# Scores of a chunked recurrence in blocks of 32 tokens: narrow diagonal products, affine maps on ScalarE, another order of heads

## The chip, the cores and the metric

The kernel runs on one core of one Trainium2 chip. The metric is device time in microseconds (us) of one execution; times are compared as medians over several runs, and each kernel also leaves one execution with a profile.

## What is computed

One layer of a decoder trunk over 1040 tokens (16 meta tokens and 1024 of the sequence) with 1024 channels in fp32: a norm, a wide projection, an HGRN2 recurrence with four heads beside a causal pooling, gates, an output projection, and a gated MLP with a causal convolution. The change lies in the recurrence. Cut to that, the reference is:

```python
f = lb + (1.0 - lb) * sigmoid(fl);  log_f = log(max(f, LOG_FLOOR))
k = (1.0 - lb) * sigmoid(-fl)
b = cumsum(log_f, axis=2)                                   # within a chunk
decay = where(causal, exp(b[t] - b[s]), 0.0)                # per channel of k
scores = einsum('bhtk,bhtsk,bhsk->bhts', q, decay, k)
o_intra = einsum('bhts,bhsv->bhtv', scores, v)
o_inter = einsum('bhtk,bhkv->bhtv', q * exp(b), state)
new_state = exp(b_last)[..., None] * state + einsum('bhsk,bhsv->bhkv', k * exp(b_last - b), v)
```

## The kernel before

Channels lie on the 128 partitions and tokens along the free axis, so a head (128 key channels) is one tile of 128x1040: q, kk (the key), f and f2 (the forget gate, twice, for a logarithm split in two ranges), b (the running sum of the logarithm, by a scan on VectorE, L632). Chunks have 128 tokens; there are NCH = 8 of them behind the meta tokens.

**Scores by levels.** A decay between two tokens must not be split into two factors that overflow. So the 128x128 causal scores of a chunk are built up by levels h = 2, 4, 8, 16, 32, 64 (LEVELS). At level h the chunk is cut into blocks of 2h tokens, and the products of a block's second half (queries) with its first half (keys) are taken, both scaled by the decay to the middle of the block. `level_in` (L669 to L681) makes the scaled tile d: a subtraction, two exponentials, two multiplies. `level_mm` (L683 to L696) multiplies: for levels 32 and 64 only the block's own quadrant, with 32 or 64 stationary columns (L691); for levels 2 to 16 the whole chunk, 128 stationary columns against the 64 queries of that level (L695), of which most products are of no use. `level_out` (L698 to L710) brings them into sc, the scores of the head (128x1024, cleared on GpSimd at L648): for levels 32 and 64 by copies (L704), below that by a copy under a mask (L710), 512 elements on each partition. The masks are made at the start (L575 to L594). Pairs of neighbouring tokens (the base, L759 to L766) come from a product of the whole chunk, 128x128 (L763), and a masked copy of 512 elements for each half of the chunks (L764).

**The steps of a head.** `head_steps` is a generator; each `h` with a number in the list ORDER runs one head on to its next yield, twelve in all: (1) the input of levels 2 and 4 and of the meta tokens, (2) meta product (L663) and level 2, (3) level 4 and the input of 8 and 16, (4) level 8, (5) level 16 and the input of 32 and 64, (6) level 32, (7) level 64 and the factors qs, kd, e1 (L726 to L745), (8) transposes of kd (L752, L755), (9) the base, (10) the states (L772 to L783), (11) scores times values and queries times state (L794 to L805), (12) the norm of the head (L809 to L817).

**The order of the work.** ORDER is a list written out by hand. F, Q, G, PV are projections of one head (or one pooling group) each, with bodies at L208 to L212 (`a` and `b` behind a letter: first and second half of the projection); after an F, `c` runs `chain_f` (L623 to L633): five element steps on VectorE (L624 to L628), two logarithms on ScalarE, an addition and the scan. `post_q` (L635) copies the queries. PP, BB and BA are the pooling and branch products, sp, sa, w smaller steps of them. Each projection's weights come through a loader three ahead, on the queue of SyncE. POOLED names the element steps that run on GpSimd instead of VectorE (such as `lq64.1`, level 64's query multiply of head 1). In this stage the order that ORDER gives is put onto the engines by the tile framework; the stages before and after (values and gates, then the output projection and the MLP) are ordered by hand. PSUM is a pool of eight banks in this stage. SBUF slots have a pitch of LP = 1088 elements.

Of the kernel before, what the change touches and what calls it, by code (L numbers as in the profile page):

```python
# [8 lines left out]
F32 = mybir.dt.float32  # L9
# [5 lines left out]
P = 128  # L15
# [25 lines left out]
LSPLIT = 2.0 ** -60  # L41
LUP = 2.0 ** 60
KT = 6
HT = 514
HN = HT - HALO
HP = 528
# [11 lines left out]
ORDER = ("F0 c0 Q0 h0 F1 h0 h0 c1 Q1 h0 h1 h0 F2 h1 h1 c2 h0 h0 Qa2 Qb2 h1 h1 h2 G2 h0 h0 h1 Fa3 h1 h2 h0 h2 Fb3 "  # L58
# [3 lines left out]
POOLED = ("e1k.0 e1k.3 kdmul.2 kdmul.3 kdsub.2 lk32.1 lk4.1 lq16.1 lq32.1 lq32.2 lq64.0 lq64.3 lq8.0 lq8.1 lq8.2 "  # L62
          "osg.2 sub2.2 sub32.1 sub8.1 wBA2 wBA6 wBA7 wBB2 wF0 wF2 wF3 wPP2 wPV0 wPV1 wQ0 wQ1 lq4.3 kdsub.1 qsmul.1 "
          "lk32.0 e1q.3 e1q.1 lq2.1 wQ2 sub2.3 rsl.0 lk32.3 lq64.1 qsmul.2").split()
TRUNC = False

CH_ALL = [(0, 348), (348, 346), (694, 346)]
# [4 lines left out]
def trunk_kernel(ctx: ExitStack, tc: tile.TileContext, x, meta_tokens, mix_norm_pre,  # L72
# [48 lines left out]
    def small(shape, name, tag, bufs=4):  # L121
        return sm.tile(shape, F32, tag=tag, name=nm(name), bufs=bufs)
# [360 lines left out]

    lb = const.tile([P, HEADS], F32, name="lb")
    oml = const.tile([P, HEADS], F32, name="oml")

    def params():
# [12 lines left out]
        dve.tensor_scalar(oml, lb, -1.0, 1.0, ALU.mult, ALU.add)  # L500


    junk_bank = bank("pj")
# [70 lines left out]

    LEVELS = (2, 4, 8, 16, 32, 64)  # L575
    masks = {}
    mbase = const.tile([P, P], U8, name="mbase")
    mtmps = slot(P + len(LEVELS) * P // 2, name="mtmps")
    mtmp = mtmps[:, :P]
    pool_e.memset(mtmp, 1.0)  # L580
# [4 lines left out]
    pool_e.tensor_copy(mbase, mtmp)  # L585
    for i, h in enumerate(LEVELS):
# [6 lines left out]
        masks[h] = const.tile([P, P // 2], U8, name=f"mask{h}")  # L593
        pool_e.tensor_copy(masks[h], mt)  # L594

    def V(c, h):
        return heads[h]["v"][:, c * P : (c + 1) * P]
# [23 lines left out]
        return lambda: chain_f(h, kk, b, f, f2)  # L621

    def chain_f(h, kk, b, f, f2):  # L623
        dve.tensor_scalar(f, f, oml[:, h : h + 1], lb[:, h : h + 1], ALU.mult, ALU.add)  # L624
        dve.tensor_scalar(kk, kk, oml[:, h : h + 1], None, ALU.mult)
        dve.tensor_scalar(f2, f, LUP, 1.0, ALU.mult, ALU.min)
        dve.tensor_scalar(f2, f2, LOG_FLOOR * LUP, None, ALU.max)
        dve.tensor_scalar(f, f, LSPLIT, None, ALU.max)  # L628
        act.activation(f2, f2, AF.Ln)
        act.activation(f, f, AF.Ln)  # L630
        eng(f"lf.{h}").tensor_tensor(f, f, f2, ALU.add)
        dve.tensor_tensor_scan(b, keep_on, f, 0.0, ALU.mult, ALU.add)  # L632
        heads[h].update(kk=kk, b=b, f=f)  # L633

    def post_q(h, pq):  # L635
        q = slot(L, name="q")
        for (lo, n), ps in zip(CH_Q, pq):
            act.copy(q[:, T0 + lo : T0 + lo + n], ps[:, :n])
        heads[h]["q"] = q

    def head_steps(h):
# [6 lines left out]
        pool_e.memset(sc, 0.0)  # L648
# [34 lines left out]
        def level_mm(lv, qk):  # L683
            ps = bank("sl")
            half = lv >= 32
            for c in range(NCH):
                t = NM + c * P
                if half:
                    for i in range(P // (2 * lv)):
                        s, n = t + 2 * lv * i, 2 * lv * i  # L690
                        pe.matmul(ps[n : n + lv, c * lv : (c + 1) * lv], qk[:, s : s + lv], qk[:, s + lv : s + 2 * lv],  # L691
                                  start=True, stop=True)
                    continue
                rhs = qk[:, t : t + P].rearrange("p (b two h) -> p b two h", two=2, h=lv)[:, :, 1, :]
                pe.matmul(ps[:, c * 64 : (c + 1) * 64], qk[:, t : t + P], rhs, start=True, stop=True)  # L695
            return ps  # L696

        def level_out(lv, ps):  # L698
            if lv >= 32:
                o3 = sc.rearrange("p (c t) -> p c t", c=NCH)  # L700
                p3 = ps[:, : NCH * lv].rearrange("p (c h) -> p c h", c=NCH)
                for i in range(P // (2 * lv)):
                    n = 2 * lv * i
                    dve.tensor_copy(o3[n : n + lv, :, n + lv : n + 2 * lv], p3[n : n + lv])  # L704
# [5 lines left out]
            dve.copy_predicated(o4, m4, p4)  # L710

# [44 lines left out]
        ktm = small([NM, P], "ktm", "ktm", 2)  # L756
        act.copy(ktm, pm[:NM, :P])
        yield
        for j in range(2):  # L759
            ps = bank("sb")  # L760
            for i in range(4):
                t = NM + (4 * j + i) * P
                pe.matmul(ps[:, i * P : (i + 1) * P], kk[:, t : t + P], q[:, t : t + P], start=True, stop=True)  # L763
            dve.copy_predicated(sc[:, j * 512 : (j + 1) * 512].rearrange("p (c t) -> p c t", c=4),  # L764
                                mbase.rearrange("p (o t) -> p o t", o=1).to_broadcast([P, 4, P]),
                                ps.rearrange("p (c t) -> p c t", c=4))  # L766
        yield


# [1031 lines left out]
```

## Time and profile before

| | us |
|---|---|
| median of 3 runs | 1330.72 (1330.1 to 1331.8) |
| the profiled execution | 1330.1 |
| its span, first to last instruction | 1328.4 |
| TensorE busy | 1317.1 |
| VectorE busy | 970.7 |
| ScalarE busy | 566.8 |
| GpSimd busy | 440.4 |

In the profile PE is TensorE's matmuls, PEld its weight loads, DVE VectorE, ACT ScalarE, POOL GpSimd, SP SyncE. A row of instructions by line reads: line, engine, operation, tile written and tiles read, shapes, how many | busy us, mean ns of one | idle us of the engine just before them, and what ended that. A row of the timeline reads: start, length, engine, line, operation, tiles, shapes, how many. A row of waits reads: who, for whom: us in total, times, longest. An fp32 matmul leaves two records. Matmuls are pipelined: the mean length of one is a latency, and the rate shows in the busy time of a row and in the starts of the timeline. The stage of the head steps runs from about 255 to 510 us.

### The profile page before, as it was taken

To read this page: it belongs to the slowest core of one execution; us is meant where nothing else is said; L and a number is where in the kernel's file an instruction comes from. 1 tells how busy PE (TensorE), PEld (TensorE's weight loads), DVE (VectorE), ACT (ScalarE), POOL (GpSimd) and SP (SyncE) were. 2 spreads that over 40 slices of the span, in tenths; PEclk is the share of its full clock that TensorE was granted. 3 is DMA by queue.
4 is the path that set the end of the run, shared out by engine and by line. 5 is a ranking of instruction groups with operands and counts; after the bars stand their busy time and mean duration, and the time that the engine had idled before them with its cause. 6 is when DMAs were issued, how large, how long until landed. Compare 5 with 4: busy or idle time off the path is not lost.

```text
span 1328.4 us, 19923 instructions
## 1 busy us (share of the span) xinstructions
PE 1317.1 (99%) x7713; PEld 1177.6 (89%) x7713; DVE 970.7 (73%) x1229; ACT 566.8 (43%) x946; POOL 440.4 (33%) x327
## 2 busy tenths in 40 slices
PE   8999999999999999999999999999999999999997
PEld 7799899999999999987898888888888888888886
DVE  6765545389968777766578999888988885455758
ACT  5553333365556575235564222322222233444443
POOL 2015421226525720061025555545555652000000
PEclk9999999999999999999999999999999999999999
DMA  7134332411011157987686776676766799666644
GB/s 272 41 110 157 124 109 99 125 50 48 19 51 35 35 170 268 350 280 257 219 300 234 183 211 188 198 205 171 178 161 142 175 246 310 215 224 223 222 174 159
DMA packets 139665, 230.38 MB, mean 173 GB/s; under 512 B 9000, under 2 KB 77196, under 8 KB 139570
## 3 DMA queue, kind: packets, MB, share of 16 engines
q1 hardware_dynamic: 127506, 204.71, 45.3%
q0 software_dynamic: 12064, 24.38, 10.8%
q8 instruction: 61, 1.00, 0.3%
q14 instruction: 34, 0.28, 0.1%
HBM read 165.56 MB, written 86.53 MB: 190 GB/s over the span
## 4 chain that ended last, share of the span: by engine, by line
PE 95%; DVE 4%; DMA 0%; ACT 0%; issue 0%; SPq 0%; DVEq 0%
PE P L311 15%; PE P L312 15%; PE P L314 15%; PE pd L188 5%; PE pd L190 5%; PE pd L189 5%; PE pm L188 2%; PE pm L189 2%; PE pm L190 2%; PE sl L695 1%; PE ppv L208 1%; PE pbb L208 1%; PE ppv L212 1%; PE pbb L209 1%; PE ppv L209 1%; PE pbb L212 1%
## 5 line engine op out<-in xcount | busy, mean ns | idle before, releaser
L312 PE MATMUL P<-v,whi 128*128 128x512 f32 (+2 forms) x408 | 140.7, 353 | 0.0
L311 PE MATMUL P<-v,whi 128*128 128x512 f32 (+2 forms) x408 | 140.7, 352 | 0.0
L314 PE MATMUL P<-v,wlo 128*128 128x512 f32 (+2 forms) x424 | 135.1, 349 | 0.0
L1535 DVE TENSOR_TENSOR rot<-wraw,rot 128x1024 fp32r<-128x1024 f32 x31 | 38.0, 1225 | 72.3 <-ACT rot L1534 72.2
L282 POOL TENSOR_TENSOR swa<-wraw,wraw 128x512 f32<-128x512 f32 x28 | 42.3, 1510 | 133.0 <-DMA wraw<-in_ffn_w_gate_dram 69.3
L311 PEld LDWEIGHTS P<-v,whi 128*128 128x128 f32 x408 | 76.7, 188 | 10.4
L312 PEld LDWEIGHTS P<-v,whi 128*128 128x128 f32 x408 | 76.6, 188 | 10.2
L314 PEld LDWEIGHTS P<-v,wlo 128*128 128x128 f32 x424 | 74.0, 188 | 10.8
L256 ACT CAST whi<-wraw 128x512 fp32r<-128x512 f32 x78 | 46.1, 618 | 87.6 <-PE P L312 64.2
L190 PE MATMUL pd<-rot 128*128 128x512 f32 x272 | 82.1, 389 | 0.0
L189 PE MATMUL pd<-rot 128*128 128x512 f32 x272 | 82.1, 389 | 0.0
L188 PE MATMUL pd<-rot 128*128 128x512 f32 x272 | 81.1, 389 | 0.1
L1534 ACT CAST rot<-wraw 128x1024 fp32r<-128x1024 f32 x31 | 32.7, 1055 | 90.8 <-PE pd L190 89.4
L256 ACT CAST whi<-swa 128x512 fp32r<-128x512 f32 x56 | 33.4, 618 | 81.9 <-PE P L312 76.2
L1463 DVE SCALAR_TENSOR_TENSOR y<-g,par,y 128x1024 f32<-128x1024 f32 x44 | 64.5, 1467 | 0.8
L257 DVE TENSOR_TENSOR wlo<-swb,whi 128x512 fp32r<-128x512 f32 x56 | 59.9, 1075 | 6.9 <-ACT whi L256 6.9
L257 DVE TENSOR_TENSOR wlo<-wraw,whi 128x512 fp32r<-128x512 f32 x74 | 62.3, 864 | 2.7 <-ACT whi L256 2.7
L256 ACT CAST whi<-swb 128x512 fp32r<-128x512 f32 x56 | 33.4, 618 | 68.6 <-PE P L312 64.2
L188 PEld LDWEIGHTS pd<-rot 128*128 128x128 f32 x272 | 51.0, 188 | 11.1 <-DVE p L1471 0.5
L189 PEld LDWEIGHTS pd<-rot 128*128 128x128 f32 x272 | 51.1, 188 | 10.6
L190 PEld LDWEIGHTS pd<-rot 128*128 128x128 f32 x272 | 51.0, 188 | 10.6
L311 PE MATMUL P<-t4h,whi 128*128 128x258 f32 (+1 forms) x196 | 57.0, 307 | 0.0
(421 smaller groups left out, 4133.0 us busy)
## 6 DMA issues: line engine op xcount, KB each, us to landing
wraw<-in_w_in_dram SPq DMA_DIRECT2D x36, 512.0 KB, 4.0
yt<-ysum SPq DMA_DIRECT2D x33, 512.0 KB, 4.5
wraw<-in_ffn_w_gate_dram SPq DMA_DIRECT2D x26, 512.0 KB, 7.3
wraw<-in_ffn_w_up_dram SPq DMA_DIRECT2D x22, 512.0 KB, 6.1
wsum<-in_ffn_w_down_dram SPq DMA_DIRECT2D x22, 512.0 KB, 9.0
wraw<-in_w_out_dram SPq DMA_DIRECT2D x18, 512.0 KB, 5.5
ysum<-ys SPq DMA_DIRECT2D x11, 768.0 KB, 7.7
sa<-sscr SPq DMA_DIRECT2D x16, 513.0 KB, 6.8
```

Of the source, the lines that this page charges most:

```text
L188: pe.matmul(ps, ahi, bhi, start=first, stop=False)
L189: pe.matmul(ps, ahi, blo, start=False, stop=False)
L190: pe.matmul(ps, alo, bhi, start=False, stop=last)
L256: act.copy(hi, src)
L257: (pool_e if 4 <= i < 2 * self.early else dve).tensor_tensor(lo, src, rr(hi), ALU.subtract)
L282: pool_e.tensor_tensor(s1, a21, a22, ALU.add)
L311: pe.matmul(d, whi[:, k, :], xh[:, c : c + w], start=(k == 0 and onto is None), stop=False, **go)
L312: pe.matmul(d, whi[:, k, :], xl[:, c : c + w], start=False, stop=False, **go)
L314: pe.matmul(x[:, o : o + w], wlo[:, k, :], xh[:, c : c + w], start=False, stop=(k == 3), **go)
L1463: dve.scalar_tensor_tensor(a, g[:, j : j + SEQ], cvw[:, j, m : m + 1], a, ALU.mult, ALU.add)
L1534: act.copy(hi, src)
L1535: dve.tensor_tensor(lo, src, rr(hi), ALU.subtract)
```

## The change

- Levels 2 to 16 and the base are taken per block of BLK = 32 tokens: for each chunk four matmuls with 32 stationary columns, their outputs on partitions 0, 32, 64 and 96, with 16 moving columns (levels) or 32 (base). The masked copies then have 128 elements (levels) or 256 (base) on each partition, and go to a tile of their own, dg (128x256, cleared on GpSimd, three buffers), from which, after the base, four copies of 32 partitions by 256 elements set the blocks onto the diagonal of sc. Three of the four copies of head 3 and all others are on VectorE; `dg1.3` is on GpSimd. The masks shrink with them.
- In chain_f the affine map of f goes to ScalarE, once plain and once scaled for f2; the multiplication of kk by 1 - lb is left out and q is scaled by it instead, in the copy out of PSUM. Two maxima and minima of f2 become one instruction.
- ORDER and POOLED change: Q2 is no longer split, PV1 is; head steps, sa and some branch products change places; `e1k.0`, `kdsub.2` and `lq64.1` go from GpSimd to VectorE. ACTED, the list of copies for ScalarE, is empty.
- The pitch LP is 1056.

```diff
+BLK = 32
-LP = 1088
+LP = 1056
-ORDER = ("F0 c0 Q0 h0 F1 h0 h0 c1 Q1 h0 h1 h0 F2 h1 h1 c2 h0 h0 Qa2 Qb2 h1 h1 h2 G2 h0 h0 h1 Fa3 h1 h2 h0 h2 Fb3 "
-         "h2 c3 h2 PVa0 h1 h1 PVb0 Q3 h1 h3 h0 h1 h2 h3 h2 h3 h1 PV1 h3 sp0 h3 sa1 PV2 h2 h2 PP0 h3 PVa3 h3 sp2 h2 "
+ORDER = ("F0 c0 Q0 h0 F1 h0 h0 c1 Q1 h0 h1 h0 F2 h1 h1 c2 h0 h0 Q2 h1 h2 G2 h1 h0 h2 h0 Fa3 h1 h0 h1 h2 Fb3 h2 c3 "
+         "h2 h1 PVa0 h1 PVb0 Q3 h1 h3 h0 h1 h2 h3 h2 h3 h1 PVa1 h3 PVb1 sp0 h3 PV2 h2 h2 PP0 h3 PVa3 sa1 h3 sp2 h2 "
...
+        dve.tensor_scalar(lbu, lb, LUP, None, ALU.mult)
+        dve.tensor_scalar(omlu, oml, LUP, None, ALU.mult)
...
-        dve.tensor_scalar(f, f, oml[:, h : h + 1], lb[:, h : h + 1], ALU.mult, ALU.add)
-        dve.tensor_scalar(kk, kk, oml[:, h : h + 1], None, ALU.mult)
-        dve.tensor_scalar(f2, f, LUP, 1.0, ALU.mult, ALU.min)
-        dve.tensor_scalar(f2, f2, LOG_FLOOR * LUP, None, ALU.max)
+        act.activation(f2, f, AF.Identity, scale=omlu[:, h : h + 1], bias=lbu[:, h : h + 1])
+        act.activation(f, f, AF.Identity, scale=oml[:, h : h + 1], bias=lb[:, h : h + 1])
+        dve.tensor_scalar(f2, f2, 1.0, LOG_FLOOR * LUP, ALU.min, ALU.max)
         dve.tensor_scalar(f, f, LSPLIT, None, ALU.max)
...
-            act.copy(q[:, T0 + lo : T0 + lo + n], ps[:, :n])
+            act.activation(q[:, T0 + lo : T0 + lo + n], ps[:, :n], AF.Copy, scale=oml[:, h : h + 1])
...
+        dg = small([P, NCH * BLK], "dg", "dg", 3)
         pool_e.memset(sc, 0.0)
+        pool_e.memset(dg, 0.0)
...
-                rhs = qk[:, t : t + P].rearrange("p (b two h) -> p b two h", two=2, h=lv)[:, :, 1, :]
-                pe.matmul(ps[:, c * 64 : (c + 1) * 64], qk[:, t : t + P], rhs, start=True, stop=True)
+                for n in range(0, P, BLK):
+                    k = qk[:, t + n : t + n + BLK]
+                    rhs = k.rearrange("p (b two h) -> p b two h", two=2, h=lv)[:, :, 1, :]
+                    pe.matmul(ps[n : n + BLK, c * BLK // 2 : (c + 1) * BLK // 2], k, rhs, start=True, stop=True)
...
-            o4 = sc.rearrange("p (c b two h) -> p c b two h", c=NCH, two=2, h=lv)[:, :, :, 1, :]
-            p4 = ps.rearrange("p (c b h) -> p c b h", c=NCH, h=lv)
-            nb = P // (2 * lv)
+            nb = BLK // (2 * lv)
+            o4 = dg.rearrange("p (c b two h) -> p c b two h", c=NCH, two=2, h=lv)[:, :, :, 1, :]
+            p4 = ps[:, : NCH * BLK // 2].rearrange("p (c b h) -> p c b h", c=NCH, h=lv)
             m4 = masks[lv].rearrange("p (o b h) -> p o b h", o=1, h=lv).to_broadcast([P, NCH, nb, lv])
             dve.copy_predicated(o4, m4, p4)
...
-        for j in range(2):
-            ps = bank("sb")
-            for i in range(4):
-                t = NM + (4 * j + i) * P
-                pe.matmul(ps[:, i * P : (i + 1) * P], kk[:, t : t + P], q[:, t : t + P], start=True, stop=True)
-            dve.copy_predicated(sc[:, j * 512 : (j + 1) * 512].rearrange("p (c t) -> p c t", c=4),
-                                mbase.rearrange("p (o t) -> p o t", o=1).to_broadcast([P, 4, P]),
-                                ps.rearrange("p (c t) -> p c t", c=4))
+        ps = bank("sb")
+        for c in range(NCH):
+            for n in range(0, P, BLK):
+                t = NM + c * P + n
+                pe.matmul(ps[n : n + BLK, c * BLK : (c + 1) * BLK], kk[:, t : t + BLK], q[:, t : t + BLK], start=True,
+                          stop=True)
+        d3 = dg.rearrange("p (c t) -> p c t", c=NCH)
+        dve.copy_predicated(d3, mbase.rearrange("p (o t) -> p o t", o=1).to_broadcast([P, NCH, BLK]),
+                            ps[:, : NCH * BLK].rearrange("p (c t) -> p c t", c=NCH))
+        for n in range(0, P, BLK):
+            r = slice(n, n + BLK)
+            o3 = sc[r].rearrange("p (c t) -> p c t", c=NCH)[:, :, r]
+            if f"dg{n // BLK}.{h}" in ACTED:
+                act.copy(o3, d3[r])
+            else:
+                eng(f"dg{n // BLK}.{h}").tensor_copy(o3, d3[r])
```

More of the change, by code (lines that the diff above doesn't have):

```diff
@@ L485, in trunk_kernel @@
     oml = const.tile([P, HEADS], F32, name="oml")
+    lbu = const.tile([P, HEADS], F32, name="lbu")
+    omlu = const.tile([P, HEADS], F32, name="omlu")
     def params():
@@ L576, in trunk_kernel @@
     masks = {}
-    mbase = const.tile([P, P], U8, name="mbase")
+    mbase = const.tile([P, BLK], U8, name="mbase")
     mtmps = slot(P + len(LEVELS) * P // 2, name="mtmps")
@@ L584, in trunk_kernel @@
                          pattern=[[2, P // 2], [1, 2]], channel_multiplier=-1)
-    pool_e.tensor_copy(mbase, mtmp)
-    for i, h in enumerate(LEVELS):
+    for n in range(0, P, BLK):
+        r = slice(n, n + BLK)
+        pool_e.tensor_copy(mbase[r], mtmp[r, r])
+    for i, h in enumerate(LEVELS[:4]):
         mt = mtmps[:, P + i * P // 2 : P + (i + 1) * P // 2]
@@ L592, in trunk_kernel @@
                              pattern=[[2 * h, P // (2 * h)], [0, h]], channel_multiplier=-1)
-        masks[h] = const.tile([P, P // 2], U8, name=f"mask{h}")
-        pool_e.tensor_copy(masks[h], mt)
+        masks[h] = const.tile([P, BLK // 2], U8, name=f"mask{h}")
+        for n in range(0, P, BLK):
+            r = slice(n, n + BLK)
+            pool_e.tensor_copy(masks[h][r], mt[r, n // 2 : (n + BLK) // 2])
     def V(c, h):
@@ L758, in head_steps @@
         yield
-        for j in range(2):
-            ps = bank("sb")
-            for i in range(4):
-                t = NM + (4 * j + i) * P
-                pe.matmul(ps[:, i * P : (i + 1) * P], kk[:, t : t + P], q[:, t : t + P], start=True, stop=True)
-            dve.copy_predicated(sc[:, j * 512 : (j + 1) * 512].rearrange("p (c t) -> p c t", c=4),
-                                mbase.rearrange("p (o t) -> p o t", o=1).to_broadcast([P, 4, P]),
-                                ps.rearrange("p (c t) -> p c t", c=4))
+        ps = bank("sb")
+        for c in range(NCH):
+            for n in range(0, P, BLK):
+                t = NM + c * P + n
[4 more added lines that the diff above has]
+                            ps[:, : NCH * BLK].rearrange("p (c t) -> p c t", c=NCH))
+        for n in range(0, P, BLK):
+            r = slice(n, n + BLK)
+            o3 = sc[r].rearrange("p (c t) -> p c t", c=NCH)[:, :, r]
[3 more added lines that the diff above has]
+                eng(f"dg{n // BLK}.{h}").tensor_copy(o3, d3[r])
         yield
```

10 lines of the change are left out of this document (6 added, 4 removed), and 4 rows, old and new, of the table ORDER.

## The prediction, made before the change was run

> **What bounds the kernel now.** I read the page first: busy times, the forty slices, the chain that ended last.
>
> ```profile
> PE 1317.1 (99%) x7713; PEld 1177.6 (89%) x7713; DVE 970.7 (73%) x1229; ACT 566.8 (43%) x946; POOL 440.4 (33%) x327
> ...
> PE   8999999999999999999999999999999999999997
> ...
> DVE  6765545389968777766578999888988885455758
> ...
> PE 95%; DVE 4%; DMA 0%; ACT 0%; issue 0%; SPq 0%; DVEq 0%
> ```
>
> TensorE (PE) is busy in every slice and carries 95% of the chain. The profiled execution took 1330.1 us around a span of 1328.4; I work against 1330.1, 0.6 under the median of the runs shown (1330.72). Since a busy PE is not a PE at its peak, the question is how densely matmuls follow each other where the change works. The busy times by stage (columns: window, length, then PE, PEld, DVE, ACT, POOL, clock, DMA share, GB/s) and PE's waits inside 255 to 470 us give:
>
> ```profile
> 255.00:280.00 25.00, 25.00 (x160) 24.89 (x158) 17.55 (x17) 12.62 (x21) 5.86 (x3) 1.00 0.23 65
> 280.00:320.00 40.00, 40.00 (x324) 39.46 (x323) 35.66 (x32) 28.37 (x46) 21.26 (x12) 1.00 0.23 67
> 320.00:360.00 40.00, 39.43 (x316) 38.51 (x314) 39.50 (x38) 23.30 (x36) 23.94 (x13) 1.00 0.05 16
> 360.00:400.00 40.00, 40.00 (x284) 39.49 (x284) 26.98 (x41) 20.17 (x37) 11.95 (x7) 1.00 0.15 42
> 400.00:440.00 40.00, 40.00 (x328) 39.54 (x327) 33.21 (x32) 25.02 (x40) 20.45 (x10) 1.00 0.09 29
> 440.00:470.00 30.00, 30.00 (x249) 29.09 (x248) 21.31 (x29) 18.17 (x32) 23.99 (x11) 1.00 0.13 38
> ```
>
> ```profile
> PE sl L691 <- ACT sg L825: 0.4, 1, 0.4
> ```
>
> This is the stage of the head steps. PE waits once, 0.4 us; the clock is granted in full. VectorE (DVE) is close behind, above all from 320 to 360 (39.50 of 40), ScalarE (ACT) and GpSimd (POOL) are not, and DMA is nearly idle. So PE's time taken out of this stage should shorten the kernel one for one, as long as DVE doesn't become what PE waits for. PE has no idle slice behind the stage in which the gain could be lost.
>
> **PE: what the change removes and adds.** Of PE's work only the scores change. Rows grouped by line and form (one fp32 matmul leaves two records):
>
> ```profile
> L695 PE MATMUL sl<-d 128*128 128x64 f32 x256 | 30.2, 274 | 0.0
> ...
> L763 PE MATMUL sb<-q,kk 128*128 128x128 f32 x64 | 8.0, 275 | 0.0
> ...
> L691 PE MATMUL sl<-d 128*32 128x32 f32 x128 | 2.8, 197 | 0.4 <-ACT sg L825 0.4
> ```
>
> L695 is levels 2 to 16: 16 groups (4 levels, 4 heads) of 8 matmuls, 16 records. L763 is the base: 4 groups of 16 records. Each group becomes 32 matmuls, so 64 records, with 32 stationary columns and 16 (levels) or 32 (base) moving ones. Four times the records, so all depends on the price of one. The mean of one, 197 ns, is a latency; the busy column shows that they overlap. The row that has almost the new form is L691 at level 32: 128x32 stationary, 32 moving, output alternating between partitions 0 and 64; only the moving width of the levels and two more output places differ. The timeline of PE gives starts, from which I take what a group occupies:
>
> ```profile
> 294.73 0.63 PE L212 MATMUL pq<-uhi,wlo 128*128 128x342 f32 x3
> 295.20 3.68 PE L695 MATMUL sl<-d 128*128 128x64 f32 x32
> 298.69 0.40 PE L208 MATMUL pf<-uhi,whi 128*128 128x348 f32 x1
> ```
>
> ```profile
> 441.70 0.65 PE L212 MATMUL ppp<-plh,wlo 128*128 128x342 f32 x3
> 442.27 0.70 PE L691 MATMUL sl<-d 128*32 128x32 f32 x32
> 442.90 0.43 PE L208 MATMUL ppv<-uhi,whi 128*128 128x348 f32 x1
> ```
>
> ```profile
> 438.98 1.95 PE L763 MATMUL sb<-q,kk 128*128 128x128 f32 x16
> 440.68 0.40 PE L208 MATMUL ppp<-plh,whi 128*128 128x342 f32 x1
> ```
>
> ```profile
> 442.27:442.77 0.50, 0.49 (x30) 0.50 (x32) 1.00 0.11 33
> ...
> 345.41:345.91 0.50, 0.49 (x31) 0.50 (x32) 1.00 0.00 0
> ```
>
> - Two old levels, 32 records, hold PE from 295.20 to 298.69: 3.49 us, 1.745 a level. An old base holds it 440.68 - 438.98 = 1.70.
> - 32 narrow records hold it 442.90 - 442.27 = 0.63. In the windows of L691 alone, 30 or 31 of them run in 0.50 us: **0.016 us a record**, the rest (about 0.12) being the way back to wide matmuls.
> - The way in: three L212 last 442.27 - 441.70 = 0.57 before the narrow group, 295.20 - 294.73 = 0.47 before the wide one, so 0.10 more.
>
> A new group standing alone: 0.10 + 0.63 + 32 x 0.016 = 1.24. Two levels side by side pay the ways in and out once: 0.10 + 0.63 + 96 x 0.016 = 2.27, or 1.13 a level. The gain is 0.50 to 0.61 a level; the groups at 295.20 and, further down, at 280.29 are pairs, so I take the middle, 0.56: 16 x 0.56 = **9.0 us**. The base: 4 x (1.70 - 1.24) = **1.8 us**. At level 2 the group follows the meta matmuls (L663), 16 columns wide, which now need no change of form behind them:
>
> ```profile
> 280.11 0.25 PE L663 MATMUL sm<-q,em 128*16 128x2 f32 x4
> 280.29 3.79 PE L695 MATMUL sl<-d 128*128 128x64 f32 x32
> ```
>
> four records hold PE 0.18 there, some 0.06 of it the way out, and the 0.10 of the way in goes too: 4 x 0.16 = **0.6 us**. Sum: 11.4 us.
>
> Can the queue feed such bursts? At 345.41 the group starts with nothing queued up (PE had just waited 0.4 us), and still 31 records start in 0.50 us; so feeding isn't the limit at this price, though a burst of 64 or 128 records isn't in the trace.
>
> Two rules of the Trainium skill bear on the price. The Trainium skill, "TensorE: Matmul & The Clock Gate", section "Wait — 56ns, not 53.3ns?", says that starts are never less than about 25 ns apart however few columns move. By it a group would be an estimated 64 x 25 ns = 1.6 us before the ways in and out, and the change would bring nothing; the trace disagrees for groups whose output alternates (0.50 us for 31). "TensorEngine Tiling (Array Packing)" of the Trainium skill, section "Theoretical Speedup", allows up to four times for 32 columns, one tile to each quarter; no run here shows four.
>
> **The other engines: cover.** DVE rows of the steps touched, and the rows that price what is new:
>
> ```profile
> L710 DVE COPY_PREDICATED sc<-mask,sl 128x512 f32<-128x512 uint8 x16 | 13.8, 863 | 6.0 <-PE sl L695 5.8
> ...
> L764 DVE COPY_PREDICATED sc<-mbase,sb 128x512 f32<-128x512 uint8 x8 | 5.8, 739 | 6.5 <-PE sb L763 6.5
> ...
> L704 DVE COPY sc<-sl 32x256 f32<-32x256 f32 x8 | 3.3, 415 | 5.3 <-PE sl L691 5.2
> ...
> L658 DVE TENSOR_TENSOR em<-em,kk 128x32 f32<-128x32 f32 x4 | 0.7, 185 | 0.3 <-ACT em L657 0.3
> ...
> L624 DVE TENSOR_SCALAR f<-f,oml,lb 128x1040 f32<-128x1040 f32 x4 | 4.6, 1141 | 13.4 <-ACT f L619 13.4
> ...
> L625 DVE TENSOR_SCALAR kk<-kk,oml 128x1040 f32<-128x1040 f32 x4 | 3.0, 752 | 0.0
> ...
> L626 DVE TENSOR_SCALAR f<-f 128x1040 f32<-128x1040 f32 x4 | 3.9, 970 | 0.0
> ...
> L627 DVE TENSOR_SCALAR f<-f 128x1040 f32<-128x1040 f32 x4 | 3.6, 910 | 0.1
> ...
> L628 DVE TENSOR_SCALAR f<-f 128x1040 f32<-128x1040 f32 x4 | 2.8, 692 | 0.0
> ...
> L731 DVE TENSOR_TENSOR kd<-b 128x1024 f32<-128x1024 f32 x2 | 2.4, 1217 | 0.0
> ...
> L745 DVE TENSOR_TENSOR kk<-kk,e 128x512 f32<-128x512 f32 x2 | 2.3, 1174 | 0.0
> ```
>
> ```profile
> L629 ACT ACT_TABLE_LOAD x4 | 5.1, 1283 | 0.1
> ...
> L630 ACT ACTIVATE f<-f 128x1040 f32<-128x1040 f32 x4 | 4.2, 1061 | 0.2 <-DVE f L628 0.2
> ```
>
> ```profile
> L648 POOL MEMSET sc<- 128x1024 f32 x4 | 3.8, 956 | 4.0 <-DVE f L631 4.0
> ```
>
> - Level masks: 128 instead of 512 elements. Between 185 (L658, 32 elements) and 863 ns; I take 300: 13.8 becomes 4.8. Base: one of 256 elements a head between the same ends, I take 420: 5.8 becomes 1.7.
> - New: 16 copies of 32x256 onto the diagonal, 15 on DVE. Priced by L704: 15 x 0.415 = 6.2.
> - Decay: L624 to L628 are 17.9 us; two maxima or minima a head remain, 8 x 0.8 = 6.4.
> - Three steps come from POOL to DVE: the kd difference of head 2 (1.2, like L731) and two multiplies of heads 0 and 1 (1.2 each, like L745): 3.6.
>
> DVE: -9.0 - 4.1 + 6.2 - 11.5 + 3.6 = about -15 us, more than PE loses. That is why I cost the change at nothing besides PE: what PE waits for moves forward further than PE does. The two affine maps go to ACT, 8 x 1.06 = 8.5 us; ACT is busy 127.6 us of these 215, so they fit; if each head's pair brought a table load of its own (L629), 4 x 1.28 = 5.1 us more of the same idle time. The scale in the copy of q is free work in an instruction that was there. POOL gains a clearing of 256 elements a head (0.24 each, a quarter of L648) and one copy and loses three steps. The clearing waits for a buffer at head 3 alone (there are three); head 0's base, which frees it, stands far ahead in the order list, so nothing is held up behind it. The one diagonal copy on POOL waits for head 3's masked base; what stands behind it there are steps of the same head's tail, late in the stage, when PE has the branch matmuls to do. SP issues the same loads, in the order of the new list, into a stage in which DMA is nearly idle. Masks and two small parameter steps stand at the start, off PE's path. In the chain from base to output, one masked copy and four copies (0.42 + 4 x 0.415 = 2.1 us) replace two masked copies (1.5): 0.6 us later per head, but the state step stands between. The reordering, taken with halves that split differently, moves the same instructions of PE, and the smaller row pitch moves nothing; a wait that these bring is a rival below. Bounds: no wait goes (0.4 at most to gain), up to a few us may come.
>
> **Rivals.**
> - *Four quarters overlap more than two.* The records of one group go to four places in turn. If twice as many run at once, 0.008 a record: a group alone is 0.10 + 0.12 + 64 x 0.008 = 0.73; gain 16 x 1.0 + 4 x 0.97 + 0.6 = 20.5 us, so **1309.6**. Against it: the two records of one matmul share a quarter and follow each other, and at level 32 they already set the pace. Chance 0.13. The second rule of the Trainium skill, above, speaks for this case.
> - *DVE takes over.* From 280 to 360, DVE works 75.2 of 80 us. If the new order needs its results sooner than the relief makes them, PE waits. If half of the gain goes that way, the time is **1325**. For: 39.50 of 40; against: DVE's own loss of work. Chance 0.13.
> - *A floor under the start of a record.* L663's four records, all to one place, take 0.18 with a way out of 0.06 to 0.12: 0.030 to 0.015 each. If the new ones have such a floor, then near its middle, at 0.024, a group costs what it did, 0.22 + 64 x 0.024 = 1.76, and the time is **1330**. Against it: 0.016 in two windows. Chance 0.06. The first rule of the Trainium skill, above, leads to this case.
> - *The quarters don't overlap at all in the new sequence* (the slower side). Then a record costs its own quarter's time, twice 0.016: a group is 0.22 + 64 x 0.032 = 2.27; 16 x 0.52 + 4 x 0.57 - 0.6 = +10 us, **1340**. It decides from (1.745 - 0.22) / 64 = 0.024 us a record on. Against it: 0.016 measured with the same columns. Chance 0.06.
>
> **How the numbers follow.** Forecast 1330.1 - 11.4 = 1318.7 against the profiled execution, 1319.3 against the median; I say **1319.3**, chance 0.62. The range, from the four-quarter case to the floor: 1310 to 1330. A measurement here tells 0.2% (2.7 us) from no change. Faster: 0.62 + 0.13 + 0.12 = 0.87; same: the floor and a little of the DVE case, 0.07; slower: 0.06.
>
> **What would show it.** Right: PE's narrow groups hold it near 1.2 us each (32 to 0.5 us), the scores' total falls by about 11 us, PE's waits between 255 and 460 stay under 1 us, DVE's busy time falls by some 15 us and ACT's rises by 8 or 9. Wrong: records over 0.024 us apart; waits of PE on masked copies, scan or level products; or records 0.008 apart, which would make the gain about double.

## The result and the profile after

The changed kernel takes **1331.89 us** (median of 20 runs, 1330.49 to 1336.51) against 1330.27 for the kernel before in the same rounds: 1.0019 times as long, interval [1.0011, 1.0027]. The forecast was 1319.3. The profiled execution is one of its longer ones: 1335.12 us, span 1333.4.

From the page of the changed kernel, the busy times, TensorE's slices and the engines' shares of the chain that ended last:

```profile
PE 1305.4 (98%) x8673; PEld 1157.9 (87%) x8673; DVE 972.5 (73%) x1234; ACT 576.0 (43%) x954; POOL 437.3 (33%) x335
...
PE   8999999998999999999999999999999999999997
...
PE 84%; DVE 7%; ACT 3%; DMA 3%; issue 2%; SPq 0%; POOL 0%; DVEq 0%; ACTq 0%
```

PE is busy for 11.7 us less and still ends later. Its share of the chain went from 95% to 84%: somewhere it is no longer PE that sets the time. The busy times by stage say where (window, length, PE, PEld, DVE, ACT, POOL, clock, DMA share, GB/s):

```profile
255.00:280.00 25.00, 25.00 (x160) 25.00 (x159) 12.81 (x13) 14.79 (x22) 6.54 (x3) 1.00 0.23 64
280.00:320.00 40.00, 33.98 (x603) 32.58 (x602) 29.95 (x30) 29.80 (x47) 19.35 (x11) 0.93 0.21 56
320.00:360.00 40.00, 38.04 (x517) 36.36 (x517) 33.20 (x39) 27.05 (x40) 17.41 (x11) 0.99 0.10 29
360.00:400.00 40.00, 36.64 (x471) 35.40 (x470) 29.05 (x39) 20.82 (x36) 13.87 (x8) 0.96 0.15 43
400.00:440.00 40.00, 38.14 (x594) 36.85 (x594) 34.39 (x37) 25.89 (x43) 19.71 (x9) 1.00 0.10 30
```

Before, PE was busy 40.00, 39.43, 40.00 and 40.00 us in the last four; now it has 6.0, 2.0, 3.4 and 1.9 us without work. No other engine is full over 40 us either, so the waits have to be read one by one. PE's waits over the whole kernel (waiting engine, tile and line, whom for: us, times, longest):

```profile
PE sl L708 <- DVE d L691: 4.8, 3, 3.4
PE pm L190 <- DVE sa L918: 3.0, 1, 3.0
PE pj L513 <- POOL ident masks.py:199: 2.0, 1, 2.0
PE sl L708 <- issue: 1.9, 2, 1.4
PE sl L702 <- DVE d L691: 1.8, 1, 1.8
PE sl L702 <- DVE d L690: 1.7, 1, 1.7
PE pf L210 <- ACT kt L767: 1.5, 1, 1.5
```

Before, the waits listed in this way were 4.0 us in all, 0.4 of them in this stage. Most of the new ones are level products (L708: levels 2 to 16; L702: 32 and 64) that wait for their input d, above all for its multiplies on VectorE (L690, L691). What the products themselves cost, and VectorE's and ScalarE's rows of the parts that changed, in the stage:

```profile
L691 DVE TENSOR_TENSOR d<-d,kk 128x512 f32<-128x512 f32 x20 | 23.2, 1164 | 5.0 <-ACT d L689 5.0
...
L690 DVE TENSOR_TENSOR d<-d,q 128x512 f32<-128x512 f32 x14 | 14.1, 1012 | 2.9 <-ACT d L688 2.9
L788 DVE COPY sc<-dg 32x256 f32<-32x256 f32 x15 | 12.9, 863 | 0.3
L708 PE MATMUL sl<-d 128*32 128x16 f32 x1024 | 12.0, 187 | 7.7 <-DVE d L691 4.8 <-issue 1.9 <-DVE d L690 1.0
...
L688 ACT ACT_TABLE_LOAD x5 | 6.4, 1283 | 0.1
...
L724 DVE COPY_PREDICATED dg<-mask,sl 128x128 f32<-128x128 uint8 x16 | 5.3, 330 | 1.8 <-PE sl L708 1.5
...
L634 ACT ACTIVATE f<-f,lbu,omlu 128x1040 f32<-128x1040 f32 x4 | 5.1, 1269 | 0.0
```

The 30.2 us of L695 became 12.0. VectorE's multiplies, for which PE waits, did not get shorter; before, they were:

```profile
L680 DVE TENSOR_TENSOR d<-d,kk 128x512 f32<-128x512 f32 x20 | 17.8, 891 | 0.1
L679 DVE TENSOR_TENSOR d<-d,q 128x512 f32<-128x512 f32 x13 | 15.6, 1203 | 0.0
```

So 33 of them took 33.4 us before, and 34 take 37.3 now. A narrow group standing alone, in PE's timeline:

```profile
421.60 0.72 PE L708 MATMUL sl<-d 128*32 128x16 f32 x64 [0.44 <-DVE d L691]
422.25 0.42 PE L214 MATMUL ppv<-uhi,wlo 128*128 128x346 f32 x1
```

and a base, which moves 32 columns:

```profile
378.20 0.76 PE L777 MATMUL sb<-q,kk 128*32 128x32 f32 x64
378.89 0.43 PE L210 MATMUL ppv<-uhi,whi 128*128 128x348 f32 x1
```

64 records hold PE 422.25 - 421.60 = 0.65 us. In such groups the first and last starts are 0.54 to 0.55 us apart, so one record takes **0.0087 us**, about half of what two places in turn took (0.016). The levels' groups also have half the moving columns of that row, but the base has all 32 and holds PE no longer to speak of (378.89 - 378.20 = 0.69 us): it is the four places, and not the smaller width, that halve the price. By such starts the sixteen wide levels and four wide bases held PE 35.3 us before (0.7 of a wait inside taken off), and the narrow ones, where nothing holds them up, 13.0: 0.67 alone, 1.24 a pair, 0.69 a base. PE's part of the gain is thus **22 us**, twice my 11.4, and none of it arrived. (The ways into the narrow form, 0.1 us each, are not in this; busy times of runs below give 21.)

One place shows how. The critical chain of the changed kernel between 281 and 320 us (start, length, what):

```profile
281.66 0.18 PE pf L211
...
284.21 0.46 ACT f L629
...
286.47 1.28 ACT L688
...
289.44 0.52 ACT d L689
289.96 1.16 ACT f L634
...
291.14 1.26 ACT f L635
...
292.42 1.28 ACT L638
...
295.78 1.25 DVE f L640
...
297.06 2.34 DVE b L641
...
302.28 3.70 DVE d L686 x2
305.99 2.23 DVE wlo L157
...
309.83 4.17 DVE d L690 x2
...
314.21 2.56 DVE d L691
...
316.90 1.94 PE sl L702 x16
```

From the end of head 1's projection (281.8) to 316.9 nothing on this chain is PE's. ScalarE does sigmoids, then, queued behind them, the exponentials of another head with a table load (L688), then the new affine maps, then a table load for the logarithms (L638); VectorE follows with sum, scan, differences, a split of weights and multiplies. Two multiplies at 309.83 take 2.1 us each, while the shortest of the same form take 0.68. PE's time around it (same columns as above):

```profile
308.00:312.00 4.00, 2.07 (x107) 1.73 (x107) 4.00 (x5) 3.46 (x6) 4.00 (x3) 1.00 0.45 131
312.00:316.00 4.00, 1.44 (x87) 1.23 (x75) 4.00 (x3) 2.37 (x6) 4.00 (x2) 0.79 0.02 4
316.00:320.00 4.00, 3.10 (x20) 3.01 (x21) 3.85 (x7) 2.08 (x4) 1.57 (x3) 0.50 0.52 140
320.00:324.00 4.00, 4.00 (x23) 4.00 (x23) 3.62 (x5) 3.94 (x5) 2.49 (x2) 0.86 0.44 122
```

VectorE is full, GpSimd works beside it, PE waits, and from about 314 to 321 the granted clock is 0.50: the waits are paid twice. "TensorE: Matmul & The Clock Gate" of the Trainium skill, section "Part 1: The HAM clock gate (the "warmup" mystery)", says that an idle window of some 3.4 us halves the clock and a busy one brings it back; the trace agrees in the lengths, with stretches at half clock of 6.8 us here and 3.4 us near 370 and 584. It doesn't quite agree in the condition: in the 3.4 us before the fall at 314 PE was not idle throughout, but ran a group of 0.73 us at 311.74.

### The profile page after: what moved, and what is told of

The parts are those of the page before. It is cut to its first block, busy times and chain, and to the rows that moved or that the text cites. A ratio compares the mean times of both kernels' runs of the same rounds, so it can differ in the third digit from the quotient of the medians.

```text
span 1333.4 us, 21871 instructions
## 1 busy us (share of the span) xinstructions
PE 1305.4 (98%) x8673; PEld 1157.9 (87%) x8673; DVE 972.5 (73%) x1234; ACT 576.0 (43%) x954; POOL 437.3 (33%) x335
## 4 chain that ended last, share of the span: by engine, by line
PE 84%; DVE 7%; ACT 3%; DMA 3%; issue 2%; SPq 0%; POOL 0%; DVEq 0%; ACTq 0%
PE P L313 15%; PE P L316 15%; PE P L314 15%; PE pd L190 5%; PE pd L191 5%; PE pd L192 5%; PE pm L190 2%; PE pm L191 2%; PE pm L192 2%; PE pv L191 1%; DVE d L686 1%; PE pv L192 1%; PE pv L190 1%; PE pq L210 1%; PE pq L211 1%
## 5 line engine op out<-in xcount | busy, mean ns | idle before, releaser
L259 DVE TENSOR_TENSOR wlo<-swb,whi 128x512 fp32r<-128x512 f32 x56 | 63.5, 1140 | 6.8 <-ACT whi L258 6.7
L258 ACT CAST whi<-swa 128x512 fp32r<-128x512 f32 x56 | 33.4, 618 | 81.2 <-PE P L314 78.3
L258 ACT CAST whi<-swb 128x512 fp32r<-128x512 f32 x56 | 33.4, 618 | 69.4 <-PE P L314 65.0
```

The lines of the kernel that those rows point to most:

```text
L258: act.copy(hi, src)
L259: (pool_e if 4 <= i < 2 * self.early else dve).tensor_tensor(lo, src, rr(hi), ALU.subtract)
```

## The experiments

I began with three theories. **P**: the shorter pitch of 1056 makes products slower that stream from SBUF. **C**: PE, quicker now, comes to the level products before VectorE has their input ready. **O**: the new order of heads makes the waits by itself. All times are medians; "before" ran beside each.

### e1, e12: the pitch

```diff
-LP = 1088
+LP = 1056
```

> The kernel before with a slot pitch of 1056 instead of 1088 and nothing else. Theory P (the pitch matters): in the changed kernel the 512-wide matmuls that read the normed input take 232 ns from start to start instead of 227, and the 1056 matmuls of the gates hold the engine 157.9 us instead of 156.7, ahead of any other part of the change; so the pitch alone should give the same 232 ns and 157.9 us and a time 2 to 4 us above the kernel before. Rival (those records were slow in that execution for another reason): 227 ns, 156.7 us, a time within 1 us.

The kernel before with this alone: **1335.81** (before 1330.16), 1.0044 [1.0032, 1.0057]. P holds, and is larger than expected: +5.6 us. Starts of 512-wide products lie 229 to 232 ns apart in place of 227 for the later tiles (t4h, t4l, zc) and 232 to 233 for the normed input; PE is busy 3.9 us longer (1321.0 against 1317.1), and its listed waits grow from 4.0 to 5.8 us in all. In e12 the normed input kept 1088:

```diff
-U0 = LP - L
+UP = 1088
+U0 = UP - L
-    def ubig(dtype, name, n=KD * LP):
+    def ubig(dtype, name, n=KD * UP):
...
```

> The kernel before with the slots of the head steps at the new pitch of 1056 columns and the normed input's tiles left at 1088: it splits the 5.6 us that the pitch of 1056 cost for both. If the cost lies with the streamed normed input (the gates' 512-wide products, 227 to 232 ns), the time is within 1.5 us of before's 1330.2. If it lies with the slots (zc, yh and yl, t1l), it is 1333 to 1336 us; evenly shared, 1332 to 1333.

**1333.19** (before 1330.31), 1.0018 [1.0009, 1.0027]: half of the cost, 2.9 us, lies with the slots, the rest with the normed input, whose products are back at 227 ns here.

### e2, e3, e4: the other parts alone

e2 has the narrow products, dg and the pitch, but the old chain_f, copy of q, ORDER and POOLED. e3 is the kernel before with the new chain_f and copy of q, e4 the kernel before with the new ORDER and POOLED; their diffs are the ones shown with the change.

> The kernel before with the narrow products alone (blocks of 32, small masks, the tile dg and its four copies, pitch 1056), with the old decay steps, the old order list and the old list of GpSimd steps. Theory C (cover): the scores' matmuls fall by some 25 us of TensorE time, and TensorE then waits for the inputs of the levels, since the list puts the products of one level right behind those of another and the wide products were the cover; time 1322 to 1334, with 15 us or more of waits between 280 and 465 us. Theory O (the new order and the moved steps make the waits): few waits, under 5 us in all, time 1305 to 1312.

> The kernel before with the decay's affine maps on ScalarE alone (and q scaled in place of kk), wide products, old order, old pitch. Theory C: TensorE hides it, within 1.5 us of the kernel before, TensorE's waits between 280 and 465 us under 1 us. Theory O: the longer way over ScalarE makes TensorE wait, 3 us slower or more.

> The kernel before with the new order list and the new list of GpSimd steps alone; wide products, old decay, old pitch. Theory C: within 2 us of the kernel before, with the wide products still covering the inputs. Theory O: 5 us slower or more, with waits of TensorE for level inputs near 310 and 366 us and for the last branch products near 580 us, as in the changed kernel.

e2: **1334.79**, 1.0028 [1.0017, 1.0040]; e3: **1330.96**, 1.0006 [0.9997, 1.0015]; e4: **1334.78**, 1.0035 [1.0022, 1.0047]. PE waits in e2 at the same kinds of places as after the change, 14.7 us between 255 and 470 against 13.7, so the narrow products bring the waits under the old order too, and O falls as the sole cause. (The pitch is in e2 as well; against e1 the narrow products alone are worth 1.0 us.) Under the wide products the affine maps cost nothing that can be told. With the wide products the new order and the new list of GpSimd steps cost 4.6 us together, between what C and O gave them: PE's listed waits are 8.5 us in e4 against 4.0 before.

### e5: the normed input's pitch given back

The diff of e12, on the changed kernel.

> The changed kernel with the old pitch of 1088 for the two big tiles of the normed input alone; all other slots keep 1056. Theory P1 (the pitch acts through the normed input's start addresses): the 512-wide matmuls that read it come back to 227 ns from 232, the gates' 1056 matmuls hold the engine 156.7 us again, and the time falls by 2 to 3 us, to about 1329.5. Rival P2 (each slot has its own part): the matmuls on other slots stay slow (zc 230, yh and yl 231 ns) and the time falls by 1 us or less.

**1330.44** (before 1330.5), 1.0004 [0.9994, 1.0013]: 1.5 us better than after by the medians, between what the two theories of its forecast gave, and the base of most of what follows.

### e6, e7, e8: is it the level inputs alone?

e6 adds the old wide products behind each narrow group, into columns that nobody reads; e7 lets the products read q in place of d, while d is still made and nothing reads it, so the scores are other ones; e8 moves halves of the projections Q2, G2 and PV0 between the head steps, on e5.

```diff
# e6
+                    pe.matmul(ps[:, 256 + (c % 4) * 64 : 320 + (c % 4) * 64], qk[:, t : t + P], rhs, start=True, stop=True)
# e7
-                level_out(lv, level_mm(lv, d))
+                level_out(lv, level_mm(lv, q))
# e8
-"F0 c0 Q0 h0 F1 h0 h0 c1 Q1 h0 h1 h0 F2 h1 h1 c2 h0 h0 Q2 h1 h2 G2 h1 h0 h2 h0 Fa3 h1 h0 h1 h2 Fb3 h2 c3 "
+"F0 c0 Q0 h0 F1 h0 h0 c1 Q1 h0 h1 h0 F2 Qa2 h1 h1 c2 h0 Qb2 h0 h1 h2 Ga2 h1 h0 Gb2 h2 h0 Fa3 h1 h0 h1 h2 Fb3 h2 c3 "
-"h2 h1 PVa0 h1 PVb0 Q3 ...
+"PVa0 h2 h1 PVb0 h1 Q3 ...
```

> The changed kernel, and behind every narrow group of levels 2 to 16 and of the base also the old wide products, into columns that nothing reads: TensorE has the old work of about 36 us again on top, while VectorE, ScalarE and GpSimd do what they do in the changed kernel. Theory C (TensorE waits for level inputs that the wide products used to cover): most of it falls into the waits, the waits between 280 and 465 us go from some 27 us to under 10 and the time rises by 6 to 16 us, to 1338 to 1348. Rival (the waits are of something that more TensorE work can't cover, such as banks or the order): the whole 36 us come on top, 1366 to 1370.

> The changed kernel, but the products of all six levels take the query tile, which is ready early, on both sides in place of the scaled tile d; d is still made in full, by the same steps, and nothing reads it. The scores are therefore not those of the reference. Theory C: the waits of TensorE for d go, the time falls by 12 to 24 us, to 1308 to 1320. Rival (the order of the steps or the throughput of VectorE sets the stage): the waits move to other operands and the time stays within 4 us of the changed kernel.

> The changed kernel with the old pitch for the normed input (as e5) and an order list that puts half a projection between head steps which stood back to back: Q2 and G2 in halves, steps of heads 0, 1 and 2 between the halves. Theory C: the waits near 310 us shrink from 6 us to 2 or less, and the time is 1320 to 1326. Rival (the chain of a head sets the stage however the projections lie, or the transfers of the branch stage do): within 3 us of e5.

e6: **1357.04**, 1.0189 [1.0174, 1.0205]; e7: **1333.93**, 1.0032 [1.0019, 1.0045]; e8: **1336.96**, 1.0043 [1.0031, 1.0056]. e6 is 25 us above the changed kernel, between the two ranges of its forecast: of the 36 us of added PE work only 11 fell into waits. That is no pure measure of the waits, since VectorE's masked copies now wait 7.7 us for the added products. In e7 the waits for d go, but PE's waits are now these:

```profile
PE pt L766 <- DVE st L804: 3.8, 1, 3.8
PE sl L702 <- DVE dg L724: 3.6, 1, 3.6
PE pm L190 <- DVE sa L918: 3.1, 1, 3.1
...
PE po L825 <- DVE st L804: 2.0, 2, 1.5
```

PE waits for banks and states that VectorE frees or makes later in its queue. e8 is 6.5 us slower than e5, which neither of its theories gave: the wait near 310 us is gone and one of 9.6 us, for kd on VectorE, stands at 331. So C in its plain form falls: whichever product is relieved, another one waits. That left **theory D**: in this stage VectorE, ScalarE and GpSimd, each in order and feeding each other, go at a pace of their own, and PE, relieved of 22 us, only waits for them.

### e9 and e16: the pace taken away

The exponentials and multiplies of the levels are left out (d holds the bare differences, so the scores are other ones), in e9 from e5, in e16 from the kernel before.

```diff
-            act.activation(db[:, :, 1, :], db[:, :, 1, :], AF.Exp)
-            act.activation(db[:, :, 0, :], db[:, :, 0, :], AF.Exp, scale=-1.0)
-            eng(f"lq{lv}.{h}").tensor_tensor(db[:, :, 1, :], db[:, :, 1, :], blocks(q, lo, lv)[:, :, 1, :], ALU.mult)
-            eng(f"lk{lv}.{h}").tensor_tensor(db[:, :, 0, :], db[:, :, 0, :], blocks(kk, lo, lv)[:, :, 0, :], ALU.mult)
```

> The changed kernel with the normed input's tiles at the old pitch (1330.4 us by itself), and with the levels' exponentials and multiplies left out: d holds the differences alone and the products read them, so the output is not the reference's. It takes 12 VectorE/GpSimd multiplies and 12 ScalarE exponentials from each head and leaves TensorE's work as it is. Theory D (the stage of the head steps goes at the pace of VectorE, ScalarE and GpSimd together, and TensorE's saved 29 us only open waits): the waits close and the time comes near TensorE's own 1305 us with the steady stage's loss of some 5 to 10 us, 1308 to 1317 us. Rival (TensorE itself is slower by something that its narrow products do to it, clock or switching): the waits may go but the time stays within 3 us of 1330.4.

> The kernel before with the levels' exponentials and multiplies left out, as in e9; the output is not the reference's. If TensorE alone set the time, nothing moves: 1328.5 to 1331 us, and e9 (1314.1) is then the change's whole gain, 16 us, with the pitch of the slots still in it. If the kernel before also waited for these steps, below 1326 us.

e9: **1314.10** against e5's 1330.44, 0.9876 [0.986, 0.9891] of before. e16: **1329.32**, 0.9989 [0.998, 0.9999]. PE's work is the same with and without these steps, so this is the pair that decides: taking them away is worth 1.0 us before the change and **16.3 us** after it. Windows of e5, then e9, then e16:

```profile
280.00:320.00 40.00, 34.02 (x601) 32.62 (x600) 30.02 (x31) 31.06 (x48) 20.65 (x11) 0.91 0.24 66
...
360.00:400.00 40.00, 36.63 (x401) 35.48 (x401) 25.95 (x37) 19.63 (x33) 12.28 (x7) 0.91 0.15 42
```

```profile
280.00:320.00 40.00, 39.35 (x651) 38.20 (x650) 21.01 (x25) 26.85 (x37) 8.54 (x5) 1.00 0.24 68
...
360.00:400.00 40.00, 38.48 (x483) 37.29 (x482) 21.18 (x34) 20.90 (x34) 9.15 (x5) 1.00 0.19 57
```

```profile
280.00:320.00 40.00, 40.00 (x324) 39.44 (x323) 25.52 (x29) 18.55 (x30) 7.64 (x4) 1.00 0.22 67
...
360.00:400.00 40.00, 40.00 (x283) 39.37 (x282) 19.56 (x30) 14.62 (x28) 7.06 (x4) 1.00 0.14 42
```

In e5 PE lacks 6.0 and 3.4 us of the 40 and runs at a clock of 0.91; in e9 it is busy 39.35 and 38.48 at full clock; in the kernel before it needed no relief. D holds, and the rival of e9, that the narrow products themselves slow PE, falls. The pair leaves out work of three engines at once, so it doesn't tell which of them sets the pace. It also gives PE's saving once more: PE is busy 1296.9 us in e9 and 1315.9 in e16, both at full clock, 19.0 less, and the slots' pitch had added 2.2 (1319.3 in e12 against 1317.1): 21 us.

### e11, e13, e15: GpSimd beside VectorE

e11 is e5 with the 18 entries of POOLED that begin with lq, lk or sub taken out, so that VectorE does them; e13 takes out the other 11 of the heads too; e15 is the kernel before without its 19 of lq, lk and sub.

```diff
-POOLED = ("e1k.3 kdmul.2 kdmul.3 lk32.1 lk4.1 lq16.1 lq32.1 lq32.2 lq64.0 lq64.3 lq8.0 lq8.1 lq8.2 osg.2 sub2.2 "
+POOLED = ("e1k.3 kdmul.2 kdmul.3 osg.2 wBA2 wBA6 wBA7 wBB2 wF0 wF2 wF3 wPP2 wPV0 wPV1 wQ0 wQ1 kdsub.1 qsmul.1 "
...
```

> The changed kernel with the normed input's tiles at the old pitch (1330.4 us), and with the levels' subtractions and multiplies (18 entries, those of lq, lk and sub) taken off GpSimd's list, so that VectorE does them all. If the speed at which VectorE works beside GpSimd (about 2.1 us for a multiply of 520 columns against 0.7 alone) is what makes it late, VectorE takes 18 more but does each faster, and the time is 1323 to 1330 us. If VectorE is late by the plain number of its instructions, the 18 moved ones (some 1 us each) make it later: 1335 to 1350 us.

> As e11 (1326.1 us), and the other 11 steps of the heads on GpSimd's list (of e1k, e1q, kdmul, kdsub, qsmul, osg, rsl and a diagonal copy) put on VectorE as well; only splits of weights stay on GpSimd. If GpSimd's work beside VectorE still costs, 1321 to 1326 us. If VectorE by now is late by its own number of instructions, 1327 to 1335 us.

> The kernel before with the levels' subtractions and multiplies (19 entries) taken off GpSimd's list. If TensorE alone set the time of the kernel before, nothing moves: 1329 to 1331.5 us. If the kernel before was already partly at the pace of VectorE beside GpSimd, 1326 to 1328.5 us, or, if VectorE becomes late, over 1332.

e11: **1326.09**, 0.9965 [0.9953, 0.9976]; e13: **1328.42**, 0.9981 [0.9972, 0.999]; e15: **1333.28**, 1.0016 [1.0007, 1.0026]. The multiplies of e5, and those of e11:

```profile
L692 DVE TENSOR_TENSOR d<-d,kk 128x512 f32<-128x512 f32 x20 | 23.2, 1162 | 5.0 <-ACT d L690 5.0
...
L691 DVE TENSOR_TENSOR d<-d,q 128x512 f32<-128x512 f32 x14 | 14.1, 1011 | 2.6 <-ACT d L689 2.6
```

```profile
L690 DVE TENSOR_TENSOR d<-d,kk 128x512 f32<-128x512 f32 x24 | 20.3, 844 | 0.0
L689 DVE TENSOR_TENSOR d<-d,q 128x512 f32<-128x512 f32 x24 | 16.4, 684 | 7.4 <-ACT d L687 7.3
```

VectorE does 48 of them in 36.7 us in place of 34 in 37.3: work that GpSimd took off VectorE made VectorE's own work as much longer. "SBUF — State Buffer" of the Trainium skill, section "Who interferes with whom", gives a reason: a VectorE instruction with two inputs in SBUF contends with a GpSimd instruction that reads SBUF; these rows agree (1011 to 684 ns). It is not a rule for the time, though: e13 goes further and is 2.3 us slower than e11 by the medians, with intervals that just overlap, and in the kernel before the same step costs 3 us (e15: a wait of 2.1 us of the base on a GpSimd step, one of 1.5 on a weight split), which I had put at nothing.

### e10, e14, e17, e18: toward a better version

e10 is e5 with the old ORDER and POOLED; e18 is e11 with the old ORDER. e14 is e11 with all sixteen diagonal copies in ACTED. e17 is e11 with LP = 1088 throughout and FM_SLOTS = 25 in place of 26, one slot given up for the larger pitch.

> The changed kernel with the old order of heads and the old list of GpSimd's steps, and with the normed input's tiles at the old pitch of 1088: narrow products and decay on ScalarE stay. If the order costs 4.6 us as it did alone with the wide products, 1326 us; if theory D holds, the order's price is mostly the same waits a second time, and the time is 1328 to 1331 us, since VectorE, ScalarE and GpSimd set the stage and their work is the same but for the lists.

> As e11 (1326.1 us), with all 16 diagonal copies on ScalarE in place of VectorE. VectorE gives up 15 copies of 0.8 us, 12 us; ScalarE takes 16. If VectorE's pace is what is left of the loss, 1318 to 1324 us. If ScalarE's order of work is as late as VectorE (the exponentials queue behind the copies), 1326 to 1332 us.

> As e11 (1326.1 us), with the slots of the head steps at the old pitch of 1088 too, which makes room for 25 slots in place of 26. If the slots' pitch costs what it cost with the wide products, 2.9 us, 1323 us; between 1322 and 1325. If the missing slot makes transfers or steps wait, 1327 to 1335 us.

> As e11 (1326.1 us), with the old order of heads (GpSimd's list stays that of e11). If the order costs by itself what it cost with the wide products, 1321.5 us; between 1320 and 1324. If the pace of VectorE and ScalarE sets the stage whatever the order, 1325 to 1329 us.

e10: **1332.09**, 1.0009 [1.0, 1.0018]; e14: **1330.88**, 0.9997 [0.9987, 1.0007]; e17: **1337.06**, 1.0045 [1.0032, 1.0058]; e18: **1326.47**, 0.9968 [0.9956, 0.998]. With the narrow products the order is worth nothing that can be told (e10 is 1.7 us above e5, e18 0.4 above e11): its 4.6 us belong to the wide ones. Taking 15 copies from VectorE makes e14 4.8 us slower than e11, so VectorE's sum of work isn't the bound; where the copies stand in ScalarE's queue counts as well (in e14 the projection pg waits 1.5 us for a copy of kt on ScalarE, L766, a wait that e11 doesn't list). e17 is 11 us slower; whether by the missing slot or by the pitch, one run with both can't tell. The best versions are e11 and e18, 0.3% faster than the kernel before; taking the levels' steps off GpSimd brought that, 4.4 us against e5.

## Why the prediction was wrong, point by point

- **PE bounds the kernel now**: right. Before the change PE alone set the time (e16: 1.0 us for all those steps).
- **PE's time goes one for one to the end, "as long as DVE doesn't become what PE waits for"**: this condition failed, and it is the step that sank the forecast. I met it with sums: VectorE loses more than PE, "that is why I cost the change at nothing besides PE". But a stage in which VectorE works 75.2 of 80 us under a full PE is one where the others end just in time. The sum of busy time is no measure of when the next input is ready: the way from a projection to its level products passes ScalarE three times and VectorE three times (sigmoid and affine map, limits, logarithm, sum and scan and difference, exponentials, multiplies), in queues shared with other heads. PE's saving arrives at once, while VectorE's relief lies in the masked copies and the maps, and the multiplies that PE waits for got no shorter (37.3 us for 34 against 33.4 for 33). Price: 16.3 us (e5 against e9).
- **VectorE loses 15 us**: mis-sized. From 255 to 470 us it went from 174.2 to 166.4 by the windows, 7.8, and some of that only moved behind 470 (35.9 to 38.6 us from there to 520); over the whole kernel it lost nothing (970.7 to 972.5). The diagonal copies took 863 ns, not 415 (6.7 us more in all), and the levels' multiplies 3.9 us more. The masked copies (330 ns against 300, 462 against 420 for the base) were about right.
- **0.016 us a record**: mis-sized, 0.0087; PE's saving is 22 us, not 11.4. The rival of four overlapping quarters had the right price and 1309.6, the time it would have given with nothing else in the way. The reason given against it, that two records of one matmul already set the pace with two quarters, was wrong. The rule in "TensorEngine Tiling (Array Packing)" of the Trainium skill, section "Theoretical Speedup", spoke for it and the runs agree as far as they go: twice the quarters, half the time. The other rule of the Trainium skill, no less than about 25 ns between starts ("TensorE: Matmul & The Clock Gate", section "Wait — 56ns, not 53.3ns?"), does not hold for these groups (8.7 ns).
- **"The smaller row pitch moves nothing"**: wrong, 5.6 us (e1), of which the slots have 2.9 (e12).
- **The reordering moves the same instructions**: true, and yet 4.6 us with the wide products (e4); nothing with the narrow ones.
- **ScalarE gains 8.5 us**: it gained 9.2. The affine maps took 1269 and 1257 ns, not 1061, and the scale in the copy of q, put at nothing, lengthened it from 445 to 540 ns, 1.1 us in all. With the wide products all this costs no time (e3); with the narrow ones the maps lie on the chain shown (289.96 to 292.40), and no run takes out them alone.
- **Rival "DVE takes over"**: the right mechanism, with the price wrong. I let it take half of the gain.

The account: 1330.3 - 22 (products) + 5.6 (pitch) = 1313.9; measured 1331.9, so 18 us are lost in waits and in the slow clock behind them, of which e9 shows 16.3 to hang on the pace of the levels' steps. e9 itself is about 3 us above 1330.3 - 22 + 2.9 = 1311.2; its trace has PE without work for 15.9 us of the span (1312.8 - 1296.9), e16's for 11.6 (1327.5 - 1315.9), so waits of some 4 us are left there and account for it. What stays open: which of the three engines sets the pace, and why e13 and e14 lose what they should have gained.

## What to carry to other kernels

An engine at 99% can hide a second chain that ends just in time; before counting a saving on the first, follow one input of its work back through every queue it passes, and compare when it is ready with when it will now be wanted. The quickest test is the one of e9 and e16: leave the second chain's work out, before and after, and see what it is worth. A step moved from VectorE to GpSimd is not free for VectorE, and a changed tile pitch is a change of its own, to be timed alone.

## What the runs showed of the hardware that was not expected

- The records of narrow fp32 matmuls (32 stationary columns) to four column quarters in turn start 0.0087 us apart on average (64 records in 0.55 us, and 0.57 with 32 moving columns), to two quarters 0.016.
- Where TensorE waited for most of some 3 us, its granted clock was halved for 3.4 or 6.8 us (0.50 in the window from 316 to 320), even with a group of 0.73 us run in between; the lone wait of 1.4 us near 411 left it at 1.00.
- A pitch of 1056 elements in place of 1088 moves starts of 512-wide products from 227 ns to 229 to 233 ns and costs 5.6 us in all; the runs don't show why.
- VectorE's multiply of 128x512 by q takes 684 ns with GpSimd off the levels' steps and 1011 on average with it, single ones 2.1 us (by kk: 844 and 1162).
